# Repeating the samples' columns on ScalarE instead of GpSimd, and emitting retention heads at a higher rate beside dense work

## The chip, the core and the metric

The kernel runs on one core of a Trainium2 chip. Its engines run side by side: TensorE (matmuls; PE in the profile, and PEld its weight loads), VectorE (DVE), ScalarE (ACT), GpSimd (POOL) and SyncE (SP), whose queue issues nearly all of this kernel's DMA transfers. The metric is the device time of one execution in microseconds, less is better.

## What is computed

The reference is one step of a two-layer decoder for 512 prompt tokens and, beside them, 8 sequences of 4 new tokens (the samples). Layer 0 mixes with sparse attention, layer 1 with retention; each is followed by an MLP with squared ReLU. Only the retention of layer 1 is touched here:

```python
def retention_mixer(h, state0, pos, w_in, w_out):
    z = h @ w_in
    q, k, v, g = jnp.split(z, [qk, 2 * qk, 2 * qk + vd], axis=-1)
    q = rotate(q, pos)
    k = rotate(k, pos) * (RET_KEY_DIM ** -0.5)
    o, S = retention_chunked(q, k, v, state0)
    o = _rms(o) * jax.nn.silu(g)
    y = o @ w_out
    return y, S
```

There are 4 heads with keys of 256 and values of 512 elements. A prompt head computes decayed scores of 512 x 512, multiplies them with the values and returns a new state of 256 x 512. A sample multiplies its 4 queries with its old state, adds the scores among its 4 tokens, and updates its state, for 8 samples and 4 heads.

## The kernel before

Activations lie transposed: 128 features on the partitions, and 544 columns, 512 of the prompt and 32 of the samples (8 x 4). Every product of float32 matrices is made of three passes over operands that are split in a high and a low part: ACT copies to the rounded type (the high part, `split_into` L678, `split_w` L477), VectorE subtracts it from the source (the low part, L679, L478), and TensorE sums high x high, high x low and low x high.

**Dense work** is the projections. `block` makes units of it: one load of 1 MB of weights into a `raw` buffer (4 of these), a split into `wh` and `wl` (2 of each), and the matmuls (`tile_of`, all recorded as L518) into a PSUM buffer `mm` (2 of these). `run` goes through a list of units. After each 12 matmuls of 272 columns it calls `tick`, and this lets the side work go on: `during` gives a list of Python generators and a rate, and each tick allows the first generator to emit instructions until the sum of the amounts it yields passes the sum of the rates. A tick stands for 1.5 us of dense work, and an amount is roughly us of side work. The order of emission is the priority by which the instructions are then laid out on the engines; each engine runs its own in the order so found, and waits for data or buffers by semaphores. So the rate decides how early in the dense work a head's instructions stand.

**Retention** has four phases, one for each head h (L1622 to L1632). Before the first, `project(0)` computes k and q of head 0 beside `values(0)`. A phase's dense work is: the gate of head h (16 ticks; the gates of heads 1 and 2 were computed earlier and are loaded by `load_gates`, after tick 4), the output projection of head h - 1 (`wout`, 16 ticks, for h > 0), and `project(h + 1)`, k and q of the next head (8 ticks each, for h < 3). Each phase thus has 32 ticks. Beside it run first `core(h)`, then `values(h + 1)`, at rate 1.1 in heads 0 to 2 and 1.3 in head 3. Before the second half of k, after tick 20, `load_values` asks for four `xs` buffers and loads the next head's values into them.

- `rotated` (L1358) rotates k or q: VectorE multiplies with cosine and sine (L1363, L1364 for the first half, rotb L1369 and rotc L1372 for the second), and GpSimd adds (L1370, L1373). For k it then calls `after_k`: the transposed prompt keys are decayed and split (kh L1395 on ACT, kl L1396 on VectorE), and the samples' 32 columns are repeated four times (krep L1401), transposed (L1405) and decayed (kf, kst).
- `values` (L1431): for each of four blocks e, VectorE scales the loaded values (L1439), GpSimd repeats the samples' 32 columns four times (vrep L1441), TensorE transposes the prompt's columns (L1445) into `pa` and the repeated ones (L1449) into `pb`, ACT and VectorE split the former into vh and vl, and ACT copies the latter to vf (L1450). After the fourth, vst is made of vf (L1453, L1455).
- `core` (L1484): the prompt's scores (L1507, a L1510), the samples' products with their states in two groups of four samples (L1533), the updates of these states (L1541, L1544, L1546), the prompt's outputs (L1563), which are multiplied with the gate (L1576), the prompt's new state (L1589, so L1593), the normalizer (L351, rw, L361, ro L363 and L364), and the normalized outputs (L1602), split on ACT (L678) and VectorE (L679) into eight `xs` buffers that the next phase's `wout` multiplies.

Buffers that the parts share: two `pa` and two `pb` in PSUM; three of tag `tz` (a, os, so, ro, rotb, rotc, gu of the gate); 28 of tag `xs`, of which the projections' operands hold 16; one each of vh, vl, kh, kl and vrep. After the last head `wout(3)` runs alone, and then the second MLP.

Of the kernel before, what the change touches and what calls it, by code (L numbers as in the profile page):

```python
# [30 lines left out]
AF = mybir.ActivationFunctionType  # L31
# [4 lines left out]
SP = 512  # L36
NB = 8
TS = 4
NS = NB * TS
# [105 lines left out]
def decoder_step(ctx, tc, x_prompt, x_sample, cache_k, cache_v, cache_kidx, state_ret, page_table,  # L145
# [5 lines left out]
    V, A, G, PE, SY = nc.vector, nc.scalar, nc.gpsimd, nc.tensor, nc.sync  # L151
# [1140 lines left out]
    GATES_KEPT = (1, 2)  # L1292
# [38 lines left out]
    with ExitStack() as st:  # L1331
# [48 lines left out]
        def project(h):  # L1380
            s = ST[h] = {"v": [], "vf": None, "g": []}

            def after_k():
                kr = s["k"]
                kh, kl = s["kd"] = [rp.tile([128, 4, 256], FR, name=n) for n in ("kh", "kl")]
                for jj in range(2):
                    ps = ps_a()
                    for j in range(2):
                        for dt in range(2):
                            PE.transpose(ps[:, 256 * j + 128 * dt:256 * j + 128 * (dt + 1)],  # L1390
                                         kr[dt][:, 128 * (2 * jj + j):128 * (2 * jj + j + 1)], ident)
                    for j in range(2):
                        jb = 2 * jj + j
                        dec = cst("kdec")[:, 4 * h + jb:4 * h + jb + 1]
                        A.activation(kh[:, jb, :], ps[:, 256 * j:256 * (j + 1)], AF.Identity, scale=dec)  # L1395
                        V.scalar_tensor_tensor(kl[:, jb, :], ps[:, 256 * j:256 * (j + 1)], dec, kh[:, jb, :].bitcast(FT),  # L1396
                                               op0=OP.mult, op1=OP.subtract)
                    yield
                krep = rp.tile([128, 2, 4, NS], FT, name="krep", tag="km", bufs=2)
                for dt in range(2):  # L1400
                    G.tensor_copy(krep[:, dt], kr[dt][:, None, SP:].to_broadcast([128, 4, NS]))  # L1401
                yield
                ps = ps_b()
                for dt in range(2):
                    PE.transpose(ps[:, 128 * dt:128 * (dt + 1)], krep[:, dt].rearrange("p r n -> p (r n)"), ident)  # L1405
                kf = rp.tile([128, 256], FT, name="kf", tag="km", bufs=2)
                V.tensor_scalar(kf, ps[:, :256], cst("kdecs")[:, h:h + 1], None, op0=OP.mult)
                kst = s["kst"] = rp.tile([128, 256], FR, name="kst", bufs=2)
                A.activation(kst, kf, AF.Copy)
                V.tensor_tensor(kst[64:128, :], kf[64:128, :], kst[64:128, :].bitcast(FT), op=OP.subtract)  # L1410

            def after_q():
                s["strip"] = rp.tile([128, 512], FT, name="strip")
                SY.dma_start(s["strip"], c_ret[h, :, :512])
                qa = qarr[h % 2]
                for dt in range(2):
                    for bb in range(2):
                        G.tensor_tensor(qa[:, dt, bb, :, 4 * bb:4 * bb + 4],
                                        s["q"][dt][:, SP + 16 * bb:SP + 16 * bb + 16].rearrange("p (j t) -> p j t", j=4),
                                        qdec[:, h, 16 * bb:16 * bb + 16].rearrange("p (j t) -> p j t", j=4),  # L1420
                                        op=OP.mult)
                yield

            return rotated(1024 + 256 * h, "kr", s, "k", after_k) + rotated(256 * h, "qr", s, "q", after_q)
# [6 lines left out]
        def values(h):  # L1431
            s = ST[h]
            for e in range(4):
                if e == 0:
                    s["v"] += [rp.tile([128, 4, 512], FR, name=n) for n in ("vh", "vl")]
                    s["vf"] = rp.tile([128, 512], FT, name="vf", bufs=1)
                (vh, vl), vf = s["v"], s["vf"]
                z = s["z"][e]
                V.tensor_tensor(z, z, RB, op=OP.mult)  # L1439
                vr = rp.tile([128, 4, NS], FT, name="vrep")  # L1440
                G.tensor_copy(vr, z[:, None, SP:].to_broadcast([128, 4, NS]))  # L1441
                yield 0.2
                pa = ps_a()
                for j in range(4):
                    PE.transpose(pa[:, 128 * j:128 * (j + 1)], z[:, 128 * j:128 * (j + 1)], ident)  # L1445
                split_into(vh[:, :, 128 * e:128 * (e + 1)], vl[:, :, 128 * e:128 * (e + 1)],
                           pa.rearrange("p (j d) -> p j d", j=4))
                pb = ps_b()
                PE.transpose(pb[:, :128], vr.rearrange("p r n -> p (r n)"), ident)  # L1449
                A.activation(vf[:, 128 * e:128 * (e + 1)], pb[:, :128], AF.Copy)  # L1450
                if e == 3:
                    vst = s["vst"] = rp.tile([128, 512], FR, name="vst", bufs=1)
                    A.activation(vst, vf, AF.Copy)  # L1453
                    for r in (1, 3):
                        V.tensor_tensor(vst[32 * r:32 * (r + 1), :], vf[32 * r:32 * (r + 1), :],  # L1455
                                        vst[32 * r:32 * (r + 1), :].bitcast(FT), op=OP.subtract)
                yield 0.6
# [13 lines left out]
        def gate(h):  # L1471
            def ev_g(i, ps):
                u = rp.tile([128, T], FT, name="gu", tag="tz", bufs=3)
                V.tensor_tensor(two(u), halves(ps), two(RB), op=OP.mult)
                g = hs_tile(FT)
                A.activation(g, u, AF.Sigmoid)
                G.tensor_tensor(g, g, u, op=OP.mult)
                ST[h]["g"].append(g)
            units = []
            for half in range(2):  # L1480
                units += dense8(w_in, 4096 + 512 * h + 256 * half, 256, ev_g)
            return units

        def core(h):  # L1484
# [74 lines left out]
            for e in range(4):  # L1559
                ps = ps_b()  # L1560
                for j in range(4):
                    for v, a in ((vh, am[0]), (vh, am[1]), (vl, am[0])):
                        PE.matmul(ps[:, SP - WJ[j]:], v[:, j, 128 * e:128 * (e + 1)], a[:, AM[j]:AM[j] + WJ[j]],  # L1563
                                  start=(j == 0 and v is vh and a is am[0]), stop=(j == 3 and v is vl))
                    if j == 1:
                        yield 1.1
                if e == 0:
                    pt = ps_a()
                    for i in range(4):
                        PE.transpose(pt[:, 128 * i:128 * (i + 1)], os_[:, 128 * i:128 * (i + 1)], ident)  # L1570
                    ptv = pt.rearrange("p (e j r) -> p e j r", e=4, j=4)
                    for bb in range(2):
                        V.tensor_copy(osT[:, :, 16 * bb:16 * bb + 16].rearrange("p e (j t) -> p e j t", j=4),
                                      ptv[:, :, :, 4 * bb:4 * bb + 4])
                g = s["g"][e]
                V.tensor_tensor(g[:, :SP], g[:, :SP], ps, op=OP.mult)  # L1576
                V.tensor_tensor(g[:, SP:], g[:, SP:], osT[:, e, :], op=OP.mult)
                sq = acc if e == 0 else tmp.tile([128, T], FT, name="sq")
                A.activation(sq[:, :SP], ps, AF.Square)
                A.activation(sq[:, SP:T], osT[:, e, :], AF.Square)  # L1580
                if e:
                    G.tensor_tensor(acc[:, :T], sq, acc[:, :T], op=OP.add)
                yield 0.65
# [28 lines left out]
        def during(units, gens, rate):  # L1612
            side.append([gens, rate, 0.0])
            run(units)
            settle()
            drain(gens)
            side.clear()
# [4 lines left out]
        for h in range(RH):  # L1622
            ahead = project(h + 1) if h + 1 < RH else []
            out = wout(h - 1) if h else []
            if h in GATES_KEPT:
                out[1]["before"] = lambda h=h: load_gates(h)
                out[2]["before"] = lambda h=h: kept_gates(h)
            gens = [core(h)]
            if ahead:
                ahead[1]["before"] = lambda h=h: load_values(h + 1)  # L1630
                gens.append(values(h + 1))
            during(([] if h in GATES_KEPT else gate(h)) + out + ahead, gens, (1.1, 1.1, 1.1, 1.3)[h])  # L1632
        final = wout(RH - 1)
        final[0]["load"]()
    mhs = ctx.enter_context(tc.tile_pool(name="mhs", bufs=16))
# [54 lines left out]
```

## Time and profile before

| | us |
|---|---|
| median of 3 runs | 1565.93 |
| lowest and highest | 1563.4, 1572.61 |
| the profiled execution | 1571.83 |
| its span, first to last instruction | 1569.9 |
| TensorE busy in the span | 1520.6 |
| retention, about | 797 to 1168 |

The profile is one execution. A table gives the busy time of each engine; windows give the same for stretches of the span with the granted clock of TensorE (1.00 is 2.4 GHz, 0.50 is 1.2 GHz); the waits say which engine stood idle until which instruction or transfer was done; a timeline lists the instructions of a stretch with the idle time before them.

### The profile page before, as it was taken

Reading aid. Unit: us, or ns where it says so; the run is one execution under the profiler, and the core shown is the slowest. Engines: PE = TensorE matmul, PEld = TensorE weight load, DVE = VectorE, ACT = ScalarE, POOL = GpSimd, SP = SyncE. Lnnn points to the kernel's source line nnn. Section 1 sums busy time; section 2 is a strip of 40 time slices with the busy share of each in tenths; the row PEclk is TensorE's granted clock in tenths of the full one; section 3 lists DMA queues with packets and bytes.
Section 4 is the critical chain, followed back from the end, with each engine's and each line's share of the span. In section 5 each row is a group of like instructions: output and inputs, shape, how many; then the busy total and the mean of one; then the engine's idle time right before and its main releaser. Section 6 shows DMA issues by size and latency. Waiting matters only on the chain.

```text
span 1569.9 us, 28355 instructions
## 1 busy us (share of the span) xinstructions
PE 1520.6 (97%) x11540; PEld 1427.3 (91%) x11540; DVE 1112.3 (71%) x2099; ACT 659.3 (42%) x1176; POOL 163.2 (10%) x165
## 2 busy tenths in 40 slices
PE   8999899999999999999999999899989999999998
PEld 6689559999999999999998988798989999999998
DVE  5599774878767766778855685867658777677663
ACT  4323663644444433555532232414236454444332
POOL 1120420100000000200012322212111000000000
PEclk9999999999999999999999989999999999999999
DMA  6433252222233223224534537282722322332212
GB/s 177 138 117 101 71 184 78 81 99 83 89 108 108 82 81 108 81 97 151 192 134 166 205 116 270 86 292 90 241 68 81 108 87 75 108 108 82 81 54 58
DMA packets 142689, 185.92 MB, mean 118 GB/s; under 512 B 12429, under 2 KB 93399, under 8 KB 142559
## 3 DMA queue, kind: packets, MB, share of 16 engines
q1 hardware_dynamic: 142490, 184.10, 35.8%
q8 instruction: 90, 1.47, 0.4%
q14 instruction: 41, 0.33, 0.1%
q10 hardware_dynamic: 68, 0.02, 0.0%
HBM read 155.03 MB, written 31.69 MB: 119 GB/s over the span
## 4 chain that ended last, share of the span: by engine, by line
PE 84%; DVE 9%; DMA 3%; ACT 2%; issue 1%; POOL 0%; SPq 0%; DVEq 0%; ACTq 0%
PE mm L518 48%; PE mm L586 22%; PE pa L586 3%; PE pb L1563 2%; PE pb L1589 1%; DVE wl L478 1%; PE pa L1533 1%; PE pb L1544 1%; PE pa L1507 1%; PE pa L1046 1%; DVE sc L813 1%; DVE m L812 1%; PE pa L1073 1%; DMA raw<-in_att_w_in_dram 1%; DVE ss L562 1%
## 5 line engine op out<-in xcount | busy, mean ns | idle before, releaser
L518 PE MATMUL mm<-xs,wh 128*128 128x272 f32 (+1 forms) x2144 | 386.9, 296 | 9.1 <-ACT xs L678 5.4
L518 PE MATMUL mm<-hs,wh 128*128 128x272 f32 x2304 | 391.8, 289 | 3.6 <-DVE x L672 2.3
L586 PE MATMUL mm<-xs,sh 128*128 128x272 f32 x1744 | 344.7, 289 | 4.8 <-ACT r L599 2.7
L518 PEld LDWEIGHTS mm<-xs,wh 128*128 128x128 f32 (+1 forms) x2144 | 318.4, 192 | 21.0 <-issue 6.6
L518 PEld LDWEIGHTS mm<-hs,wh 128*128 128x128 f32 x2304 | 327.9, 188 | 6.5 <-DVE x L672 2.9
L586 PEld LDWEIGHTS mm<-xs,sh 128*128 128x128 f32 x1744 | 276.5, 189 | 8.3 <-ACT r L602 3.5
L477 ACT ACTIVATE wh<-raw 128x1024 fp32r<-128x1024 f32 x139 | 146.6, 1056 | 317.1 <-PE mm L518 294.8
L586 PE MATMUL mm<-xs,sl 128*128 128x272 f32 x912 | 262.6, 289 | 0.0
L672 DVE TENSOR_TENSOR x<-mm,x 128x544 f32<-128x544 f32 x176 | 127.2, 723 | 165.9 <-PE mm L518 164.9
L518 PE MATMUL mm<-hs,wl 128*128 128x272 f32 x1152 | 240.3, 288 | 0.0
L518 PE MATMUL mm<-xs,wl 128*128 128x272 f32 (+1 forms) x1072 | 233.4, 294 | 0.0
L518 PEld LDWEIGHTS mm<-hs,wl 128*128 128x128 f32 x1152 | 181.8, 188 | 0.2
L478 DVE TENSOR_TENSOR wl<-raw,wh 128x1024 fp32r<-128x1024 f32 x131 | 164.1, 1254 | 22.3 <-ACT wh L477 14.5
L518 PEld LDWEIGHTS mm<-xs,wl 128*128 128x128 f32 (+1 forms) x1072 | 174.5, 191 | 4.9 <-issue 3.2
L586 PEld LDWEIGHTS mm<-xs,sl 128*128 128x128 f32 x912 | 172.3, 189 | 0.0
L678 ACT ACTIVATE sh<-ss 128x512 fp32r<-128x512 f32 x152 | 95.6, 630 | 149.8 <-PE mm L586 148.8
L679 DVE TENSOR_TENSOR sl<-ss,sh 128x512 fp32r<-128x512 f32 x152 | 104.2, 687 | 28.4 <-PE mm L586 27.4
L678 ACT ACTIVATE sh<-raw 128x512 fp32r<-128x512 f32 x114 | 72.0, 632 | 101.2 <-PE mm L586 82.6
L679 DVE TENSOR_TENSOR sl<-raw,sh 128x512 fp32r<-128x512 f32 x114 | 78.1, 685 | 13.3 <-PE mm L586 12.2
L586 PE MATMUL pa<-xs,sh 128*128 128x272 f32 x304 | 60.0, 288 | 0.0
L679 DVE TENSOR_TENSOR hs<-r,hs 128x544 fp32r<-128x544 f32 x64 | 46.1, 720 | 16.0 <-ACT hs L678 15.9
L1546 DVE SCALAR_TENSOR_TENSOR raw<-raw,pb 128x512 f32<-128x512 f32 x64 | 43.1, 683 | 17.0 <-PE pb L1544 14.5
(357 smaller groups left out, 1894.8 us busy)
## 6 DMA issues: line engine op xcount, KB each, us to landing
raw<-in_mlp_w_in_dram SPq DMA_DIRECT2D x32, 1024.0 KB
raw<-in_mlp_w_out_dram SPq DMA_DIRECT2D x32, 1024.0 KB
raw<-in_ret_w_in_dram SPq DMA_DIRECT2D x24, 1024.0 KB
raw<-in_state_ret_dram SPq DMA_DIRECT2D x32, 512.0 KB
out_dram<-raw SPq DMA_DIRECT2D x32, 512.0 KB
raw<-in_ret_w_out_dram SPq DMA_DIRECT2D x8, 1024.0 KB
raw<-in_att_w_in_dram SPq DMA_DIRECT2D x7, 1024.0 KB
kept<-r SPq DMA_DIRECT2D x24, 272.0 KB
```

Of the source, the lines that this page charges most:

```text
L477: A.activation(h, view, AF.Copy)
L478: eng.tensor_tensor(l, view, h.bitcast(FT), op=OP.subtract)
L518: PE.matmul(ps[:m, c, :HALF], w[:, k, m * t:m * (t + 1)], x[c] if isinstance(x, tuple) else x[:, HALF * c:HALF * (c + 1)], start=(k == 0 a ...
L562: V.tensor_tensor(t, a, b, op=OP.add)
L586: PE.matmul(ps, a[:, i, :], b, start=(first and i == 0 and j == 0), stop=(i == 3 and j == 2), skip_group_check=True)
L672: V.tensor_tensor(two(xT[m]), halves(ps), two(xT[m]), op=OP.add)
L678: A.activation(dst_h, src, AF.Copy)
L679: V.tensor_tensor(dst_l, src, dst_h.bitcast(FT), op=OP.subtract)
L812: V.max(out=m8, in_=sc)
L813: V.match_replace(out=sc, in_to_replace=m8, in_values=sc, imm_value=TAKEN)
L1546: V.scalar_tensor_tensor(sl, sl, gam4[h], pu, op0=OP.mult, op1=OP.add)
L1563: PE.matmul(ps[:, SP - WJ[j]:], v[:, j, 128 * e:128 * (e + 1)], a[:, AM[j]:AM[j] + WJ[j]], start=(j == 0 and v is vh and a is am[0]), stop ...
```

## The change

Two copies in retention, krep and vrep, move from GpSimd (`G.tensor_copy`) to ScalarE (`A.activation` with `AF.Copy`). The rates of the four phases become 1.4, 1.4, 1.4 and 1.8. As the gate's tiles of a head could now be asked for before they are emitted, `core` yields 1.0 until there are enough of them.

```diff
@@ after_k, in project @@
                 krep = rp.tile([128, 2, 4, NS], FT, name="krep", tag="km", bufs=2)
                 for dt in range(2):
-                    G.tensor_copy(krep[:, dt], kr[dt][:, None, SP:].to_broadcast([128, 4, NS]))
+                    A.activation(krep[:, dt], kr[dt][:, None, SP:].to_broadcast([128, 4, NS]), AF.Copy)
@@ values @@
                 vr = rp.tile([128, 4, NS], FT, name="vrep")
-                G.tensor_copy(vr, z[:, None, SP:].to_broadcast([128, 4, NS]))
+                A.activation(vr, z[:, None, SP:].to_broadcast([128, 4, NS]), AF.Copy)
@@ core, for each e, before the outputs are multiplied with the gate @@
+                while len(s["g"]) <= e:
+                    yield 1.0
                 g = s["g"][e]
@@ the phases @@
-            during(([] if h in GATES_KEPT else gate(h)) + out + ahead, gens, (1.1, 1.1, 1.1, 1.3)[h])
+            during(([] if h in GATES_KEPT else gate(h)) + out + ahead, gens, (1.4, 1.4, 1.4, 1.8)[h])
```

## Rows read from the trace of the kernel before

**Rows 1.** The page's first part: busy us (share of the span) x instructions of each engine.

```profile
PE 1520.6 (97%) x11540; PEld 1427.3 (91%) x11540; DVE 1112.3 (71%) x2099; ACT 659.3 (42%) x1176; POOL 163.2 (10%) x165
```

**Rows 2.** Windows of the span (us from its start: length, then busy us and number of instructions of PE, PEld, DVE, ACT and POOL, the granted clock of TensorE, the DMA engines' busy share and GB/s): head 0 up to its end, the stretch between heads 0 and 1, between 1 and 2, between 2 and 3, after head 3, and two of them in other limits.

```profile
797.00:899.00 102.00, 101.26 (x760) 93.36 (x760) 64.28 (x109) 28.66 (x53) 26.48 (x28) 1.00 0.48 165
899.00:914.00 15.00, 10.95 (x71) 9.64 (x70) 14.31 (x27) 7.63 (x18) 8.03 (x9) 0.66 0.32 110
987.00:1000.00 13.00, 8.95 (x72) 7.73 (x71) 12.86 (x22) 9.15 (x21) 6.68 (x9) 0.87 0.33 104
1089.00:1099.00 10.00, 8.69 (x59) 4.37 (x58) 9.09 (x21) 4.77 (x10) 0.30 (x1) 1.00 0.30 107
1154.00:1168.00 14.00, 9.81 (x56) 9.39 (x56) 7.54 (x12) 3.90 (x6) 0.00 (x0) 0.76 0.22 75
897.00:919.00 22.00, 17.95 (x118) 16.13 (x117) 19.75 (x38) 10.94 (x23) 8.03 (x9) 0.77 0.32 108
985.00:1005.00 20.00, 15.95 (x118) 14.20 (x117) 19.23 (x38) 10.65 (x23) 6.68 (x9) 0.91 0.39 122
```

**Rows 3.** The timeline of TensorE's matmuls between heads 0 and 1, and one line from the start of head 2's phase: start, duration, instruction, number, and in brackets the idle time before it and what ended it.

```profile
899.28 0.63 PE L361 MATMUL pa<-rw,ident 128*128 128x136 f32 x4
900.31 0.60 PE L1390 MATMUL pa<-ident,kr 128*128 128x128 f32 x4
...
903.98 0.47 PE L1449 MATMUL pb<-ident,vrep 128*128 128x128 f32 x1 [2.52 <-POOL vrep L1441]
905.37 1.27 PE L518 MATMUL mm<-xs,wh 128*128 128x272 f32 x4 [0.48 <-ACT xs L678]
907.32 0.47 PE L1449 MATMUL pb<-ident,vrep 128*128 128x128 f32 x1 [0.67 <-POOL vrep L1441]
...
910.35 1.11 PE L518 MATMUL mm<-xs,wh 128*128 128x272 f32 x4
...
1001.05 0.66 PE L518 MATMUL mm<-xs,wh 128*128 128x272 f32 x4
```

**Rows 4.** Who waited for whom, TensorE, 797 to 1168 us: waiting instruction, what it waited for, us in total, times, the longest.

```profile
PE mm L518 <- ACT xs L678: 5.4, 3, 3.1
PE pb L1449 <- POOL vrep L1441: 4.6, 4, 2.5
PE pb L1544 <- DVE vst L1455: 1.1, 1, 1.1
```

**Rows 5.** The timeline of VectorE between heads 0 and 1, and two lines of it between heads 1 and 2.

```profile
900.44 0.43 DVE L364 COPY ro<-pb 128x272 f32<-128x272 f32 x1
900.79 1.22 DVE L478 TENSOR_TENSOR wl<-raw,wh 128x1024 fp32r<-128x1024 f32 x1
901.92 0.72 DVE L1372 TENSOR_TENSOR rotc<-mm,rot 128x544 f32<-128x544 f32 x1
902.56 1.22 DVE L1602 TENSOR_TENSOR xs<-xs,ro 128x544 f32<-128x544 f32 x1
...
990.91 0.43 DVE L364 COPY ro<-pb 128x272 f32<-128x272 f32 x1
...
992.24 1.85 DVE L1602 TENSOR_TENSOR xs<-xs,ro 128x544 f32<-128x544 f32 x1
```

**Rows 6.** The timeline of ScalarE between heads 0 and 1.

```profile
904.49 0.28 ACT L1450 ACTIVATE vf<-pb 128x128 f32<-128x128 f32 x1 [2.34 <-PE pb L1449]
904.67 1.74 ACT L678 ACTIVATE xs<-xs 128x544 fp32r<-128x544 f32 x3
```

**Rows 7.** The timeline of GpSimd: late in head 0, between heads 0 and 1, and at the start of head 3.

```profile
878.17 0.53 POOL L1401 COPY krep<-kr 128x128 f32<-128x128 f32 x2
...
900.79 2.40 POOL L1370 TENSOR_TENSOR qr<-qr,rotb 128x544 f32<-128x544 f32 x1
903.15 0.78 POOL L1441 COPY vrep<-xs 128x128 f32<-128x128 f32 x1
...
1098.70 1.36 POOL L1477 TENSOR_TENSOR xs<-xs,gu 128x544 f32<-128x544 f32 x1 [12.10 <-ACT xs L1476]
```

**Rows 8.** Groups of GpSimd's instructions, 797 to 1160 us: line, operation, tiles, shapes, number, busy us, mean ns of one, idle us before them and its releasers.

```profile
L1441 POOL COPY vrep<-xs 128x128 f32<-128x128 f32 x16 | 8.2, 511 | 61.4 <-DVE xs L1439 35.9 <-PE pb L1449 25.5
L1401 POOL COPY krep<-kr 128x128 f32<-128x128 f32 x8 | 2.1, 291 | 0.0
```

**Rows 9.** The same for ScalarE, shapes kept apart: the high part of the smallest block of scores.

```profile
L678 ACT ACTIVATE amh<-a 128x128 fp32r<-128x128 f32 x4 | 1.2, 294 | 0.0
```

**Rows 10.** The same for VectorE: the outputs' products, their low parts, and the scaling of the values.

```profile
L1602 DVE TENSOR_TENSOR xs<-xs,ro 128x544 f32<-128x544 f32 x16 | 13.2, 883 | 0.1
L679 DVE TENSOR_TENSOR xs<-xs 128x544 fp32r<-128x544 f32 x12 | 8.5, 733 | 0.1
L1439 DVE TENSOR_TENSOR xs<-xs,RB 128x544 f32<-128x544 f32 x15 | 10.5, 723 | 5.1 <-DMA xs<-kept 5.1
```

**Rows 11.** Windows as in rows 2, of TensorE's dense matmuls (L518) alone: from the first matmul of a core to its first L1563, in heads 0 and 3.

```profile
829.00:876.00 47.00, 38.46 (x272) 1.00 0.65 225
1090.00:1129.60 39.60, 27.11 (x197) 1.00 0.56 193
```

**Rows 12.** The timeline of the SP queue: the issue of the loads of head 1's values.

```profile
861.89 1.89 SPq L1429 DMA_DIRECT2D xs<-kept  x4
```

## The prediction

> **What bounds the kernel now.** I read the table of engines first. TensorE is busy 1520.6 of 1569.9 us [rows 1], so only its idle time and its slow clock can be won back. The edits lie in retention, so I cut that stage, 797 to 1168 us, into windows [rows 2]. Inside a head TensorE hardly pauses: 101.26 of 102 us up to 899. The pauses lie between heads: from 899 to 914 it is idle 15 - 10.95 = 4.05 us, from 987 to 1000 4.05 us, from 1089 to 1099 1.31 us, and from 1154 to 1168, after the last head, 4.19 us, 13.6 us in all. Three of these windows have a mean granted clock of 0.66, 0.87 and 0.76, so 68%, 26% and 48% of them passed at the lower level (1.2 GHz); that with the pause of 1.31 us has 1.00. Four dense matmuls span 0.66 us at full clock and 1.11 at the lower level [rows 3], so 41% of the busy time there is lost: 0.68 x 10.95 x 0.41 = 3.1 us, 0.26 x 8.95 x 0.41 = 1.0 us, 0.48 x 9.81 x 0.41 = 1.9 us. With the idle time that makes 19.6 us, the most that smoother heads can give.
>
> Next I asked the waits what ends those pauses: 5.4 us ACT's split of the outputs (xs L678), 4.6 us GpSimd's repeated values (vrep L1441), 1.1 us the last product of the values (vst) [rows 4]. The timelines of the boundary at 900 us show how [rows 3, 5 to 7]. VectorE has the normalizer (ro L364) ready at 900.87, then runs a weight split (1.22) and a rotation (0.72), and starts the outputs' first product (L1602) at 902.56, done at 903.78. ACT splits that output only at 904.67: it stood 2.34 us behind vf, which waited for TensorE's transpose, which waited 2.52 us for the vrep of 903.15, which stood on GpSimd behind a rotation of 2.40 us. Dense matmuls resume at 905.37, and at 907.32 TensorE waits 0.67 us more for the last vrep.
>
> **The change, part by part.** *Copies to ScalarE.* 16 vrep and 8 krep copies leave GpSimd, which spent 8.2 + 2.1 us on them [rows 8]. The trace has no ScalarE copy of this pattern; the nearest, 128x128 from SBUF, takes 0.294 us (amh) [rows 9]. I take that: 24 x 0.294 = 7.1 us on ACT, six copies or 1.8 us a head, at a boundary where ACT is busy 10.94 of 22 us [rows 2]. The ends are 0 (hidden in that idle time) and 7.1 us (each in front of a split that TensorE waits for); I take 0, since the vf behind each vrep on ACT cannot start sooner anyway. Queued behind a copy that must wait (for VectorE's L1439, or GpSimd's rotated k) are ACT's weight splits. What it gives: at 900 ACT's 904.67 - 903.78 = 0.9 us and TensorE's 0.67, so 1.6 us. Of the four waits for vrep, 4.6 us, these two boundaries' other two make 4.6 - 2.52 - 0.67 = 1.4 us; at 990 the product starts late anyway (992.24) [rows 5], so I count 1.0. At 1090 nothing waits for vrep; a shorter GpSimd queue gives perhaps 0.5. Together 3.1 us, between 0 and 4.6.
>
> One rule would make this more. The rows have the outputs' products at 0.883 us in the mean, against 0.733 for the split of like shape, and vrep at 0.511 against krep's 0.291 for one size [rows 8, 10]. The Trainium skill, page "SBUF — State Buffer", section "Who interferes with whom", says that a VectorE instruction with two SBUF inputs and a GpSimd instruction that reads SBUF lock each other out, and that ScalarE waits for nobody; by that rule all 10.3 us of copies could come off VectorE's waiting too, and the sum would be up to 10.3 us lower, an estimate from that page. I give it nothing, since the rotations, GpSimd's longer reads, stay where they are.
>
> *Rates.* The yields of a core add up to 4.6 + 0.3 + 9.8 + 1.0 + 7.0 + 5.2 = 27.9 where the outputs are emitted, and 1.0 more to its end. A phase has 32 ticks. At 1.1 the outputs fall on tick 26 and the next head's values on 27 to 29; at 1.4 on 20 and 21 to 23. No instruction is added; only places in the order change. Does the rate hold a core back now? Between head 0's first core matmul (829) and its first L1563 (876) lie 15.7 units, 14.3 ticks at 1.1 of 12 matmuls each, 171 dense matmuls; 272 ran there. In head 3, at 1.3, 15.7 / 1.3 x 12 = 145 are due and 197 ran [rows 11]. Cores run behind their rate, held by states and VectorE, so inside a core a higher rate gives 0. The gain is at the boundary, where outputs and values now stand well ahead of the decayed keys (ticks 26 to 29) and q's rotation (32). At 900 a weight split and a rotation, 1.69 us, go ahead of the products; at 990 ro is ready at 991.34 and the product starts 0.9 us later [rows 5]. What goes first there was also ready first, so order alone mends about half: 0.8 and 0.4 us, and half of the 1.1 us for vst at 1090, 0.6. Together 1.8 us; the bounds are 0 and 3.7.
>
> *Clock.* The two pauses shrink to 4.05 - 1.6 - 0.8 = 1.65 us and 4.05 - 1.0 - 0.4 = 2.65 us. One of 1.31 us lost no clock, those of 4.05 us lost 3.1 and 1.0; between these I interpolate: 0.88 x 3.1 + 0.51 x 1.0 = 3.2 us, between 0 and 4.1. *The guard* costs nothing at 1.4: the fourth gate exists on tick 16, when the core at 22.06 / 1.4 asks for it. At 1.8 it makes head 3's core wait from tick 13 to 16, covered by dense work up to tick 32; without that cover it is 3 ticks of 1.5 us. The 4.19 us at the end I leave: head 3 is not held by its rate.
>
> **The sum.** 3.1 + 1.8 + 3.2 = 8.1 us. The profiled execution took 1571.83 us, 1.93 more than its span and 5.90 more than the median of the runs, 1565.93. So 1563.7 for an execution like it, and 1557.8 for the median, which I predict. 0.5%, 7.8 us, is about what a measurement of this kernel can tell from no change.
>
> **The rivals.** *Every boundary closes.* If VectorE's queue clears sooner and the last core, emitted at 1.8, also ends before its dense work, all 19.6 us come back: 1546.3. For it speaks that most of VectorE's late work at a boundary depends on the outputs or values that now come first; against it, the counts in [rows 11].
>
> *Nothing: the chain of cores closes up again.* A core starts when its predecessor's tiles are free, and its first 15.7 units took 47 us whatever the dense work did [rows 11]. If TensorE resumes 3 us sooner at a boundary, it runs out of dense work sooner at the next. Then only the copies' 3.1 us remain, in part: 1563, between 1558 and 1573. For it speaks that cores are behind their rate; against it, that a core's second half shares TensorE with dense work and speeds up when that is gone.
>
> *Slower: values and keys arrive late.* Buffers of one tag seem to be handed out in the order of emission: k's second block is transposed at 900.31, though k was ready when its copies ran at 878.17, and it runs just after the normalizer's transposes (899.28), emitted before it; at 1098.70 a gate had kept GpSimd waiting 12.10 us, its tz buffer being behind the core's three [rows 3, 7]. At 1.1 the next values are asked for after tick 20, before the outputs (26); at 1.4 the eight output tiles (20) come first. Sixteen of 28 xs tiles hold operands, so the values' loads would wait for this head's gates, that is for the boundary, where before they ran at 861.89 [rows 12]. Likewise k's rotations (tick 24) come to stand behind so and ro in tz. That moves 4 x 0.723 + 2 x 0.72 = 4.3 us of VectorE's work [rows 5, 10] into stretches where it is busy 19.75 of 22 and 19.23 of 20 us [rows 2]. It decides if the core waits for it and it exceeds the slack there, 2.25 and 0.77 us: at three boundaries 3 x 4.3 = 13 us, 1579; with the slack used some 8 us, 1574. Against it: the decayed keys wait for the same end of the core, and its successor needs more than the values.
>
> **Chances.** The forecast 0.38, with its own range 1550 to 1560; every boundary closed 0.11; nothing 0.32; slower 0.19. So faster 0.48, same 0.33, slower 0.19, as a tenth of the forecast lies inside the limit and a tenth of the second rival beyond it. The range reaches from below the closed case, whose clock may give a little more, to between the two prices of the slow one: 1542 to 1577.
>
> **What would show it.** Right: no vrep or krep on GpSimd, ACT copies near 0.29 us, no wait of L1449 for GpSimd; the first output split within 2 us of ro; the clock near 1.00 in the window that answers to 899 to 914; L1439 still ahead of the boundary. Wrong: L1439 and the values' loads inside the boundary, VectorE full there for over 22 us, dense matmuls waiting for weights or mm buffers, pauses over 4 us.

## The result and the profile after

The change makes the kernel slower. After takes 1585.63 us in the median of 4 runs (1581.63 to 1587.81), before, run beside it, 1566.08 us (4 runs): a ratio of 1.0116, with a 95% interval of 1.0079 to 1.0153, or 18 us (12 to 24). The forecast was 1557.8, its range ended at 1577, and "slower" had a chance of 0.19. The profiled execution of after took 1587.81 us. Lines of `core` behind the guard stand two higher in its profile: L1602 of before is L1604, so L1593 is L1595.

Up to 797 us the two traces run alike. To compare what follows, take the stretch from there to the start of the last head's normalized outputs: before, then after (length; busy us of PE, PEld, DVE, ACT, POOL; granted clock; DMA share; GB/s).

```profile
797.00:1157.50 360.50, 348.02 (x2527) 313.87 (x2526) 246.27 (x430) 106.78 (x194) 87.13 (x86) 0.98 0.51 171
```

```profile
797.00:1172.20 375.20, 352.31 (x2522) 312.42 (x2520) 249.26 (x430) 111.82 (x217) 78.50 (x62) 0.98 0.49 164
```

The loss is there: 375.2 - 360.5 = 14.7 us of the 15.8 by which the spans differ. TensorE is idle 22.89 us instead of 12.48, 10.4 more, and busy 4.3 more; the mean granted clock is 0.98 in both. What follows answers to [rows 2]: the boundaries between heads, and the end of head 3.

```profile
890.00:915.00 25.00, 21.84 (x157) 20.15 (x156) 24.04 (x37) 8.45 (x17) 10.30 (x8) 1.00 0.36 121
985.00:1000.00 15.00, 8.08 (x37) 6.90 (x36) 13.44 (x23) 3.88 (x8) 7.49 (x7) 0.72 0.30 99
1075.00:1105.00 30.00, 22.17 (x174) 19.34 (x173) 26.39 (x48) 13.40 (x30) 10.29 (x9) 0.99 0.39 125
1168.00:1184.00 16.00, 11.64 (x69) 11.20 (x68) 7.90 (x13) 4.02 (x6) 0.00 (x0) 0.79 0.19 67
```

The first boundary is mended as the forecast wished: 3.16 us idle against 4.05, clock 1.00 against 0.66. The second got worse, 6.92 us against 4.05, with a clock of 0.72, and the third much worse, 7.83 us against 1.31. The waits of TensorE, 797 to 1180 us, answer to [rows 4]:

```profile
PE mm L518 <- ACT xs L678: 6.4, 2, 4.3
PE mm L518 <- DVE xs L679: 4.6, 3, 2.2
PE pb L1544 <- DVE km L1541: 3.3, 1, 3.3
PE mm L518 <- DVE qr L1364: 2.5, 3, 1.0
PE pa L361 <- DVE rw L338: 2.0, 2, 1.0
PE mm L518 <- DVE rotc L1372: 1.4, 1, 1.4
...
PE pb L1449 <- ACT vrep L1441: 0.9, 1, 0.9
```

The wait for vrep did go, from 4.6 to 0.9 us. In its place stand longer waits for the outputs' splits (L678 6.4 us for 5.4, L679 4.6 for 1.1), one of 3.3 us instead of 1.1 for the first state update (L1544), and two kinds of which before had next to nothing (0.7 us): dense matmuls whose `mm` buffer a rotation has not emptied (L1364, L1372), and the normalizer (L361). VectorE between heads 1 and 2, against [rows 5], shows where these come from:

```profile
988.43 0.72 DVE L1369 TENSOR_TENSOR rotb<-mm,rot 128x544 f32<-128x544 f32 x1 [0.74 <-DMA out_dram<-so]
989.60 0.72 DVE L1372 TENSOR_TENSOR rotc<-mm,rot 128x544 f32<-128x544 f32 x1 [0.44 <-DMA out_dram<-so]
990.24 0.43 DVE L364 COPY ro<-pb 128x272 f32<-128x272 f32 x1
990.77 3.64 DVE L1604 TENSOR_TENSOR xs<-xs,ro 128x544 f32<-128x544 f32 x4
...
999.83 0.73 DVE L1439 TENSOR_TENSOR xs<-xs,RB 128x544 f32<-128x544 f32 x1
```

k's rotations wait for the store of so, and the values' scaling L1439 comes 9 us behind the outputs' first product. In before it ran at 949.1, 43 us ahead of it. The SP queue issues the loads of head 1's values here (three of the four), against 861.89 in [rows 12]:

```profile
902.44 1.59 SPq L1429 DMA_DIRECT2D xs<-kept  x3
```

What held them is in the waits of the SP queue, 797 to 1180 us, in after and then in before:

```profile
SPq L1429 <- DVE xs L679: 32.9, 12, 8.4
```

```profile
SPq L1429 <- PE mm L518: 3.1, 5, 1.0
```

All twelve loads of after wait for VectorE's low part of an output (L679), the last instruction that reads the buffer of its gate. So the buffers are handed out as the slower rival had it: the outputs, emitted first, took the free ones, and the values get those that the outputs' splits give back. Before has no such wait.

So the next core starts late. Its first scores, in after and then in before (the counts at the end of a line depend on the window asked for):

```profile
929.64 2.52 PE L1507 MATMUL pa<-qr,kr 128*128 128x512 f32 x6
1020.15 1.88 PE L1507 MATMUL pa<-qr,kr 128*128 128x512 f32 x4
1105.42 1.91 PE L1507 MATMUL pa<-qr,kr 128*128 128x512 f32 x2
```

```profile
918.41 1.88 PE L1507 MATMUL pa<-qr,kr 128*128 128x512 f32 x4
1004.58 3.17 PE L1507 MATMUL pa<-qr,kr 128*128 128x512 f32 x8
1089.96 1.98 PE L1507 MATMUL pa<-qr,kr 128*128 128x512 f32 x4
```

11.2, 15.6 and 15.5 us later. At the first boundary TensorE had dense work meanwhile and stood idle for no more than the 3.16 us above. I read it so that this work is then missing later, which no run shows by itself: from 988.95 us TensorE has nothing to run for 4.30 us. Why its busy time rose by 4.3 us the trace does not tell.

Each copy takes about what was estimated (against [rows 8, 9]); groups of ScalarE, 797 to 1190 us:

```profile
L1441 ACT ACTIVATE vrep<-xs 128x128 f32<-128x128 f32 x16 | 4.9, 308 | 14.6 <-DVE xs L1439 14.6
L1401 ACT ACTIVATE krep<-kr 128x128 f32<-128x128 f32 x8 | 2.4, 304 | 8.1 <-POOL kr L1370 7.8 <-POOL kr L1373 0.3
```

### The profile page after: what moved, and what is told of

It is laid out like the page before. It is cut to its first block, busy times and chain, and to the rows that moved or that the text cites. A ratio compares the mean times of both kernels' runs of the same rounds, so it can differ in the third digit from the quotient of the medians.

```text
span 1585.7 us, 28389 instructions
## 1 busy us (share of the span) xinstructions
PE 1524.8 (96%) x11540; PEld 1426.7 (90%) x11540; DVE 1116.9 (70%) x2099; ACT 664.8 (42%) x1200; POOL 154.5 (10%) x141
## 4 chain that ended last, share of the span: by engine, by line
PE 83%; DVE 10%; ACT 2%; DMA 2%; issue 2%; POOL 0%; SPq 0%; DVEq 0%; ACTq 0%; POOLq 0%
PE mm L518 47%; PE mm L586 21%; PE pa L586 3%; PE pb L1563 2%; PE pa L1507 1%; PE pb L1591 1%; PE pa L1046 1%; DVE wl L478 1%; PE pa L1533 1%; PE pb L1544 1%; DVE sc L813 1%; DVE m L812 1%; PE pa L1073 1%; DVE xs L1604 1%; DVE sl L679 1%
## 5 line engine op out<-in xcount | busy, mean ns | idle before, releaser
L518 PE MATMUL mm<-xs,wh 128*128 128x272 f32 (+1 forms) x2144 | 387.3, 296 | 18.8 <-ACT xs L678 6.4
L518 PE MATMUL mm<-hs,wh 128*128 128x272 f32 x2304 | 391.7, 289 | 3.7 <-DVE x L672 2.3
L518 PEld LDWEIGHTS mm<-xs,wh 128*128 128x128 f32 (+1 forms) x2144 | 317.0, 192 | 33.1 <-issue 7.5
L518 PEld LDWEIGHTS mm<-hs,wh 128*128 128x128 f32 x2304 | 327.9, 188 | 6.4 <-DVE x L672 3.0
L518 PE MATMUL mm<-hs,wl 128*128 128x272 f32 x1152 | 240.3, 288 | 0.0
L518 PE MATMUL mm<-xs,wl 128*128 128x272 f32 (+1 forms) x1072 | 232.6, 293 | 0.0
L518 PEld LDWEIGHTS mm<-hs,wl 128*128 128x128 f32 x1152 | 181.7, 188 | 0.2
L518 PEld LDWEIGHTS mm<-xs,wl 128*128 128x128 f32 (+1 forms) x1072 | 174.0, 191 | 2.7 <-issue 1.5
L678 ACT ACTIVATE sh<-ss 128x512 fp32r<-128x512 f32 x152 | 95.6, 630 | 150.1 <-PE mm L586 149.2
L679 DVE TENSOR_TENSOR sl<-ss,sh 128x512 fp32r<-128x512 f32 x152 | 104.3, 688 | 28.7 <-PE mm L586 27.7
L678 ACT ACTIVATE sh<-raw 128x512 fp32r<-128x512 f32 x114 | 72.0, 632 | 100.7 <-PE mm L586 82.6
L679 DVE TENSOR_TENSOR sl<-raw,sh 128x512 fp32r<-128x512 f32 x114 | 78.3, 687 | 13.2 <-PE mm L586 12.1
L679 DVE TENSOR_TENSOR hs<-r,hs 128x544 fp32r<-128x544 f32 x64 | 46.2, 722 | 16.0 <-ACT hs L678 15.9
```

Of the source, the lines that this page charges most:

```text
L518: PE.matmul(ps[:m, c, :HALF], w[:, k, m * t:m * (t + 1)], x[c] if isinstance(x, tuple) else x[:, HALF * c:HALF * (c + 1)], start=(k == 0 a ...
L678: A.activation(dst_h, src, AF.Copy)
L679: V.tensor_tensor(dst_l, src, dst_h.bitcast(FT), op=OP.subtract)
```

## The experiments

Theory A was the slower rival: buffers are handed out in the order of emission, so that at the higher rates values and keys come late. Theory B: the copies on ScalarE stand in front of splits. Theory C: the rates as such move the core's work to a bad place, whatever the buffers do. Ratios are to before, run beside each kernel, with 95% intervals; 0.1% is 1.6 us.

**copies_only**: after with the rates of before.

```diff
-            during(([] if h in GATES_KEPT else gate(h)) + out + ahead, gens, (1.4, 1.4, 1.4, 1.8)[h])
+            during(([] if h in GATES_KEPT else gate(h)) + out + ahead, gens, (1.1, 1.1, 1.1, 1.3)[h])
```

> The 24 copies on ScalarE with the rates of before (1.1, 1.1, 1.1, 1.3). Theory A (the loss comes from the order in which buffers are handed out at the higher rates): the copies are no part of the loss, so the time is that of before less up to 3 us, 1562 to 1567. Theory B (the copies stand on ScalarE in front of splits that TensorE waits for): most of the 19.5 us appear here, 1575 to 1585.

1568.38 us, ratio 0.9996 (0.9979 to 1.0014): no cost and no gain of the copies can be seen. The interval ends at a gain of 3.3 us, so it leaves the forecast's 3.1 just possible; the waits show why little of it came:

```profile
PE mm L518 <- ACT xs L678: 5.5, 3, 3.1
PE pb L1449 <- ACT vrep L1441: 2.6, 4, 0.9
PE pa L1445 <- DVE vl L679: 2.4, 1, 2.4
PE mm L518 <- DVE xs L679: 1.8, 2, 1.1
PE pa L1445 <- DVE kl L1396: 1.3, 1, 1.3
```

vrep is waited for 2.0 us less, but TensorE then waits 2.4 + 1.3 us (0.5 in before) for VectorE's splits, which empty the `pa` buffers of the transposes. On VectorE they stand behind the outputs:

```profile
898.16 3.80 DVE L1604 TENSOR_TENSOR xs<-xs,ro 128x544 f32<-128x544 f32 x4
901.89 0.47 DVE L1396 SCALAR_TENSOR_TENSOR kl<-pa,cr,kh 128x256 fp32r<-128x256 f32 x1
902.28 0.68 DVE L679 TENSOR_TENSOR vl<-pa,vh 128x512 fp32r<-128x512 f32 x1
```

**rates_only**: after with both copies back on GpSimd.

```diff
-                    A.activation(krep[:, dt], kr[dt][:, None, SP:].to_broadcast([128, 4, NS]), AF.Copy)
+                    G.tensor_copy(krep[:, dt], kr[dt][:, None, SP:].to_broadcast([128, 4, NS]))
...
-                A.activation(vr, z[:, None, SP:].to_broadcast([128, 4, NS]), AF.Copy)
+                G.tensor_copy(vr, z[:, None, SP:].to_broadcast([128, 4, NS]))
```

> The rates of after with the 24 copies left on GpSimd. Theory A: 1584 to 1590, as slow as after or a little slower. Theory B: 1560 to 1570.

1584.98 us, ratio 1.0110 (1.0075 to 1.0146), as after. Theory B falls: the rates, with the guard that goes with them, are the loss.

**values_early** and **values_late** move one thing, the place where the values are asked for: in after ahead of the outputs again, in before behind them.

```diff
@@ values_early, on after @@
-                ahead[1]["before"] = lambda h=h: load_values(h + 1)
+                ahead[0]["before"] = lambda h=h: load_values(h + 1)
@@ values_late, on before: the line above goes, and in core @@
                 s["o"].append((oh_, ol_))
+            if h + 1 < RH:
+                load_values(h + 1)
```

> After, but the next head's values are asked for one weight block earlier, on tick 16, so that their four xs tiles are handed out ahead of the eight output tiles again; VectorE's order has L1439 back inside the core, while k's rotations still come behind so and ro in tz. Theory A: L1439 runs some 25 to 30 us before the outputs again; if the xs tiles carry most of the loss 1565 to 1571, if the tz tiles carry it 1580. Theory C (it is not the buffers: at 1.4 a core's own work is emitted too early against the dense work, so that the next core starts late whatever the values do): 1582 to 1587, with the next core still starting 10 to 15 us later than in before.

> Before, with one edit: the next head's values are asked for right behind the emission of the outputs, so that at the old rates too the output tiles come first in xs. GpSimd's copies, the rates and the place of k's rotations stay. Theory A, xs part: L1439 moves behind the outputs and the time rises by 8 to 15 us, to 1574 to 1581. Theory A with the loss in tz, and theory C: 1566 to 1569.

values_early: 1573.92 us, ratio 1.0032 (1.0015 to 1.0048), so 1.16 - 0.32 = 0.84% of the loss goes. values_late: 1583.76 us, ratio 1.0086 (1.0056 to 1.0115): at the old rates, and with the old copies, the late values alone cost 13.5 us. The two agree. The starts of the cores point the same way. Counted from the first core's first scores, the next cores begin 89.6, 175.7 and 261.1 us later in before, 101.3, 191.8 and 277.1 in after, 94.4, 180.4 and 267.6 in values_early, and 94.7, 185.2 and 272.5 in values_late. So values_early takes back more than half of the delay, and some 5 to 6.5 us of it stay with the rates of 1.4. The waits of values_late:

```profile
PE mm L518 <- ACT xs L678: 10.8, 3, 4.4
PE mm L518 <- DVE xs L679: 4.3, 3, 2.2
PE pa L1445 <- DVE xs L1439: 3.0, 1, 3.0
PE pa L361 <- DVE rw L338: 2.4, 1, 2.4
```

and TensorE between heads 0 and 1, against [rows 3]:

```profile
899.80 0.63 PE L361 MATMUL pb<-rw,ident 128*128 128x136 f32 x4
900.27 0.60 PE L1390 MATMUL pa<-ident,kr 128*128 128x128 f32 x4
905.28 1.27 PE L518 MATMUL mm<-xs,wh 128*128 128x272 f32 x4 [4.41 <-ACT xs L678]
```

In before the values' transposes stood between the normalizer and the dense matmuls that need the outputs. Here nothing stands there, and the transposes follow when the dense work has resumed. The granted clock in the windows of the three boundaries, 0.66, 0.68 and 0.68, against 0.66, 0.87 and 1.00 in [rows 2]:

```profile
899.00:914.00 15.00, 9.55 (x50) 8.99 (x49) 12.89 (x18) 4.92 (x8) 6.53 (x7) 0.66 0.42 144
987.00:1003.00 16.00, 8.18 (x41) 6.88 (x40) 13.09 (x24) 5.29 (x10) 5.33 (x7) 0.68 0.40 132
1091.00:1101.00 10.00, 5.99 (x31) 5.13 (x30) 7.79 (x12) 3.38 (x7) 1.92 (x3) 0.68 0.66 217
```

**no_scale** asks whether the price of the late values is VectorE's time, as the rival had it.

```diff
-                V.tensor_tensor(z, z, RB, op=OP.mult)
```

> After without VectorE's product of the values with RB (12 instructions of 0.72 us, 2.9 us a head): the values stay unscaled, everything else as in after, their loads still inside the boundary. If VectorE's work moved into the boundary is the price (the term of 4.3 us a head in the slower rival): 6 to 10 us below after, 1574 to 1579. If the late loads are the price and not VectorE's work: within 4 us of after.

1583.58 us, ratio 1.0100 (1.0075 to 1.0125), 2.5 us below after by the ratios, within the error of both. 12 x 0.72 = 8.6 us of VectorE's work went from the boundaries and most of the loss stayed: the lateness costs, not this work. The loads still wait for the outputs' splits there, 32.7 us in all. (values_early speaks against theory C in the same way: the rates stay at 1.4 there, and most of the loss is gone.)

**keys_behind** holds the core back until k's rotation is emitted; **early_strip** frees the rotations of the store of so by giving so another buffer.

```diff
@@ keys_behind, in core, ahead of the decayed keys @@
+            while h + 1 < RH and not ST.get(h + 1, {}).get("turned"):
+                yield 1.0
@@ early_strip, on values_early @@
-                so = rp.tile([128, 512], FT, name="so", tag="tz", bufs=3)
+                so = rp.tile([128, 512], FT, name="so", tag="strip", bufs=1)
```

> After, but the core waits, ahead of its decayed keys, until k's second rotation of the next head has been emitted (tick 24), so that its two tz tiles are handed out before so and ro again, and with that the values' xs tiles before the outputs'. Rates and copies as in after. Theory A (buffers' order): the 0.32% that values_early had left come back too, ratio to before 0.997 to 1.001, and no wait of rotb or rotc for the store of so. Theory C (the rates as such cost the rest): 1.002 to 1.005, as values_early.

> values_early with one more edit: so takes the buffer of the strip (read only at a core's start) instead of a tz buffer, so that k's rotations have no store of so ahead of them. If the tz buffers carry the 0.32% that values_early had left: ratio 0.998 to 1.001, no wait of rotb or rotc for a store. If not the buffers but the place in VectorE's order carries it (at 1.4 the core's end is emitted ahead of the rotations, and VectorE's order still has k's rotations next to q's): 1.002 to 1.005 as values_early.

keys_behind: 1579.02 us, ratio 1.0066 (1.0047 to 1.0085), outside both expectations. The edit also moves the decayed keys, the normalizer and the outputs to tick 24 and later, so it does not test the rotations alone. The late values are not what it pays: their loads start at 861.16 us, and the next cores begin 89.3, 179.0 and 267.0 us after the first. TensorE waits for the outputs' splits instead, 10.3 us in all where before has 5.4 + 1.1:

```profile
PE mm L518 <- DVE xs L679: 6.1, 3, 2.5
PE mm L518 <- ACT xs L678: 4.2, 3, 2.1
```

Why these waits grew so much stays open. early_strip: 1574.89 us, ratio 1.0036 (1.0020 to 1.0052), as values_early. Its rotations wait for no store any more (2.3 us in values_early), and nothing is won, so the `tz` half of the rival is wrong as a price. k's rotations still come late (between heads 1 and 2 at 980.04 us, against 961.35 in before). I put that down to their place in VectorE's order, which no run isolates.

**slow_early_strip**: the two edits of early_strip at the rates of before (1.1, 1.1, 1.1, 1.3).

> The same two edits (values asked for on tick 16, so out of tz) and the copies on ScalarE, at the rates of before. The buffers had no late handout at these rates, so by theory A nothing is won: 0.997 to 1.001, as copies_only. If freeing tz lets the rotations or gates run earlier: below 0.997.

1569.74 us, ratio 0.9993 (0.9976 to 1.0009): at these rates neither the buffers nor asking for the values 4 ticks sooner makes a difference that can be seen.

**last_only**, **rate_12**, **rate_13**, **early_last13** differ in rates alone: (1.1, 1.1, 1.1, 1.8), (1.2, 1.2, 1.2, 1.3), 1.3 for all, and values_early with (1.4, 1.4, 1.4, 1.3). All have the copies on ScalarE.

> The copies on ScalarE, the rates of before for heads 0 to 2, and 1.8 instead of 1.3 for head 3. Theory A: the last head has no next values or keys, so nothing changes: ratio 0.998 to 1.001. Rival (the last head's higher rate costs the rest by its wait for the fourth gate or by an uncovered end): 1.002 to 1.005, with the pauses at the end of head 3 longer than 4.2 us.

> The copies on ScalarE, rates 1.2, 1.2, 1.2, 1.3: outputs on tick 24, still behind the values' loads of tick 20 and beside k's rotations of tick 24. Theory A (only the order of handing out counts): 0.998 to 1.002, as copies_only. If the loss grows with the rate itself: a third of it, 1.003 to 1.005.

> The copies on ScalarE, 1.3 for all four heads. Outputs on tick 22, behind the values' loads (20) but ahead of k's rotations (24): VectorE's order has k's rotations next to q's as at 1.4, which at 1.2 they were not. If that place of the rotations carries the rest: 1.001 to 1.004, clearly over the 0.9988 of rate 1.2. If not: 0.998 to 1.001.

> values_early with head 3 at 1.3 instead of 1.8. If the last head's rate carries the 0.32 to 0.36% that values_early and early_strip had left: 0.998 to 1.001. If the first three heads carry it: 1.002 to 1.004.

| kernel | us | ratio | interval |
|---|---|---|---|
| last_only | 1571.23 | 1.0010 | 0.9996 to 1.0025 |
| rate_12 | 1567.37 | 0.9988 | 0.9974 to 1.0003 |
| rate_13 | 1571.19 | 1.0010 | 0.9995 to 1.0025 |
| early_last13 | 1571.62 | 1.0015 | 0.9999 to 1.0030 |

The loss does not grow with the rate: at 1.2 there is none, at 1.3 hardly any, and at 1.4 (with 1.8 for the last head) over 1%, where the outputs come ahead of the values (tick 20). Only rate_12 decides between its two expectations, for theory A; the other three lie between theirs or at the edge. The last head's 1.8 costs 0.14% by last_only against copies_only and 0.17% by early_last13 against values_early, twice the same sign but each within its error. rate_13 lies 0.22% over rate_12, at the edge of the error. The rest of 0.3% may thus be shared by the last head and by rates of 1.3 and more in the others; the runs do not resolve it.

**relief** gives two of four output products to GpSimd, on copies_only.

```diff
-                V.tensor_tensor(g, g, ro, op=OP.mult)
+                (G if e % 2 else V).tensor_tensor(g, g, ro, op=OP.mult)
```

> The copies on ScalarE with the rates of before, and two of the four output products with ro (L1604, e = 1 and 3) on GpSimd instead of VectorE. copies_only took the waits for vrep from 4.6 to 2.6 us and gained nothing, as TensorE then waited 2.4 us for VectorE's split of the values. If VectorE's queue is what holds the boundary: 1.6 us less in it a head, 2 to 6 us below copies_only. If the chain from the normalizer to the split is: GpSimd's longer product makes it 0 to 4 us slower.

1573.78 us, ratio 1.0016 (0.9999 to 1.0033): nothing won; 0.2% above copies_only is within the error. The groups show it, VectorE's in copies_only, then VectorE's and GpSimd's in relief:

```profile
L1604 DVE TENSOR_TENSOR xs<-xs,ro 128x544 f32<-128x544 f32 x16 | 13.9, 929 | 0.1
```

```profile
L1604 DVE TENSOR_TENSOR xs<-xs,ro 128x544 f32<-128x544 f32 x8 | 11.9, 1531 | 0.1
L1604 POOL TENSOR_TENSOR xs<-xs,ro 128x544 f32<-128x544 f32 x8 | 15.0, 1899 | 14.4 <-DVE ro L364 14.4
```

Eight products on VectorE take 11.9 us where in copies_only sixteen took 13.9.

**half_gates**, **half_copies**, **half_after**: two of the four gates of heads 1 and 2 are computed in their own phase, ahead of the dense work that needs the outputs. half_copies adds the copies on ScalarE. half_after adds the whole change, at rates of its own (in its expectation) and with a wait in `values` until the loads are emitted. The diff is half_gates on before; the edits that load and keep two gates instead of four are left out.

```diff
-        for t in list(range(4, 16, 2)) + [16 + 4 * h + i for h in GATES_KEPT for i in (0, 2)]:
+        for t in list(range(4, 16, 2)) + [16 + 4 * h + i for h in GATES_KEPT for i in (0,)]:
...
-            for half in range(2):
+            for half in range(1 if h in GATES_KEPT else 0, 2):
...
-            during(([] if h in GATES_KEPT else gate(h)) + out + ahead, gens, (1.1, 1.1, 1.1, 1.3)[h])
+            during(gate(h) + out + ahead, gens, (1.1, 0.9, 0.9, 1.3)[h])
```

> Before, but two of the four gates of heads 1 and 2 are computed in their own phase, ahead of the dense work that needs the last head's outputs (rates 0.9 there, as the phases become 40 ticks). If a boundary costs because TensorE has no dense work that is independent of the outputs (the one boundary with a gate ahead, head 3's, paused 1.31 us and kept its clock, the two others 4.05 us each): these two pauses shrink to 1.5 to 2.5 us with the clock near 1.0, minus the dense work that is no longer saved by the seven products of eight: 1 to 5 us below before. If the chain of the core sets the end anyway: 0 to 5 us slower.

> half_gates with the 24 copies on ScalarE, its rates kept. TensorE's pauses at the boundaries are gone there, so the copies have nothing to win: 0.991 to 0.996, as half_gates. If GpSimd's shorter queue lets the next core start sooner: below 0.991.

> half_gates with the change on top: copies on ScalarE, and rates at which the outputs again come ahead of the values' loads at all three boundaries (1.4, 1.15, 1.15, 1.8 for phases of 32, 40, 40 and 32 ticks). If the late values cost because TensorE then has nothing between the normalizer and the dense work that needs the outputs: the gates give it that, so at most half of the 1.16% remains, ratio to before 0.993 to 0.999. If late values cost by themselves (the next core starts late and TensorE pays it wherever): 1.003 to 1.006.

half_gates: 1561.56 us, ratio 0.9934 (0.9912 to 0.9955). half_copies: 1558.68 us, ratio 0.9920 (0.9899 to 0.9942), the fastest of all, 12.6 us below before; the 0.14% to half_gates is less than the error. Its boundaries:

```profile
876.00:894.00 18.00, 18.00 (x156) 17.68 (x155) 16.16 (x28) 11.87 (x25) 5.31 (x6) 1.00 0.20 74
959.00:984.00 25.00, 25.00 (x205) 24.95 (x204) 23.42 (x36) 13.66 (x28) 8.08 (x8) 1.00 0.30 96
1053.00:1077.00 24.00, 24.00 (x207) 23.55 (x206) 22.02 (x34) 13.85 (x29) 8.99 (x8) 1.00 0.29 99
```

All three are without a pause and at full clock. VectorE is nearly as full as in before (16.16 of 18 us and 23.42 of 25, against 19.75 of 22 and 19.23 of 20 in [rows 2]), but TensorE has something else to do. The gates' dense work comes out of an earlier stage, so the gain of the boundaries alone is not separated; over the whole span TensorE is idle for 43.5 us in half_copies and 44.2 in half_gates, against 49.3 in before. half_after: 1569.17 us, ratio 0.9997 (0.9981 to 1.0014), between the two expectations. On top of half_copies the change costs 0.77% (error 0.28) instead of 1.16% (0.37). So the cover takes perhaps a third of its price, which the errors do not tell from nothing; most of the price it does not reach. The next cores start at 902.4, 997.4 and 1090.4 us against 894.4, 984.6 and 1077.3 in half_copies, and TensorE stands in other places, in front of the scores too (L1510 here is L1507):

```profile
PE pa L1510 <- DVE kl L1396: 2.9, 1, 2.9
PE mm L518 <- DVE xs L679: 2.2, 1, 2.2
PE mm L518 <- ACT xs L678: 2.1, 1, 2.1
```

## Why the prediction was wrong

- *Copies, their cost* (0.294 us each, hidden): right; 0.308 and 0.304 us, and no loss to be seen in copies_only.
- *Copies, their gain* (3.1 us): not seen. copies_only gives 0.6 us, between a gain of 3.3 and a loss of 2.2. The waits for vrep did shrink. The step counted them as gained without asking what is late next: VectorE's splits, behind the outputs, end the pause at the same time. The sentence that by the rule of the Trainium skill (page "SBUF — State Buffer", section "Who interferes with whom") up to 10.3 us more could come from the copies finds no support: the outputs' products took 0.929 us in copies_only and 0.920 in after, against 0.883 in [rows 10], and 0.819 in values_late, where the copies stay on GpSimd.
- *Order* (1.8 us): right where it was looked at. The outputs' first product starts at 897.79 and 990.77 instead of 902.56 and 992.24 [rows 5]. The failing step is that the forecast's sum counted these and put at nothing what the outputs were moved past, the values' loads and the rotations. Moving the loads behind the outputs alone cost 13.5 us (values_late).
- *Clock* (3.2 us): what the first boundary got back (1.00 for 0.66), the second lost again (0.72 for 0.87); the mean over the stage is 0.98 in both.
- *The slower rival*: its place was right, and so was the handing out of buffers. L1439 and the loads stand inside the boundary, the rotations wait for so, VectorE is busy for 24.04 of 25 and 26.39 of 30 us, as its signs said; the idle time exceeds 4 us at the second and third boundary, not at the first. Its price of 13 us came near the 13.5 of values_late, but for a wrong reason: it counted 4.3 us of VectorE's work a head, and no_scale shows that such work is not the price. With late values the loads, scaling, transposes and splits come behind the outputs instead of beside the core; values_late shows TensorE without work while it waits for the outputs, and in after the next core starts 11 to 16 us later.
- *The chance of 0.19*: the error that mattered. The late values were seen and weighed too low, on the sentence "the decayed keys wait for the same end of the core, and its successor needs more than the values". The rows above show the successor late by up to 15.6 us. The order of emission had been worked out, and the handing out of buffers had evidence in [rows 3]. (The gate at 1098.70 in [rows 7] shows only that GpSimd was idle until the gate's sigmoid, not which buffer that stood behind.) For a core that starts on time in spite of late values no row was given.
- *The guard*: no run isolates it at 1.4. At 1.8 the last head may cost some 2 us, not resolved.

What stays open: how the price of the late values divides between missing cover (perhaps a third, by half_after) and the late start of the cores; what exactly the last 0.3% at 1.4 is; and why TensorE waits longer for the outputs' splits in keys_behind.

## What to carry to other kernels

When a change emits work sooner, list what it passes on every shared ring of buffers, not only on the engines: the one who now asks second waits for the first one's readers, and here moving four loads a head behind the outputs cost 13.5 us, and from 1.3 to 1.4 was the step past it. A wait that a change removes is worth only the distance to the next wait behind it, so look for that before booking the gain. Where an engine stands idle at a boundary, independent work placed there (half of two gates, 0.7 to 0.8%) was worth more than shortening the chain it waits for (copies_only and relief, nothing to be seen).

## What the runs showed of the hardware

Moving half of a VectorE product to GpSimd bought little: in relief VectorE's own mean rose from 0.929 to 1.531 us, and GpSimd's took 1.899. The Trainium skill, page "SBUF — State Buffer", section "Who interferes with whom", says that a VectorE instruction with two SBUF inputs and a GpSimd instruction that reads SBUF exclude each other, and these rows agree with it. GpSimd's copies of 128 columns showed no such price on VectorE's products: taking all 24 away left them at 0.93 us, no less than the 0.883 of before.
